# Order of the score visits in a hybrid attention layer: pattern 1 in front of the joint pattern, with a new table of priority shifts

## The chip, the cores and the metric

The kernel runs on one core of a Trainium2 chip. The core has TensorE (PE in the profile, PEld its weight loads), VectorE (DVE), ScalarE (ACT), GpSimd (POOL) and SyncE (SP), which here issues nearly all DMAs. The metric is the device time of one execution in microseconds; lower is better. Before the change the median of three runs is 1198.13 us.

## The reference, cut to what matters

One decoder layer on x of 2048 tokens by 1024 columns. A norm and an input projection give q, k, v and a gate for 12 heads of 64, and the four inputs of a gated convolution of width 256. Each head attends in three dilated windows, whose outputs are combined by the softmax of their log-sums:

```python
DILATED_PATTERNS = ((128, 1), (512, 4), (2048, 16))
...
for window, dilation in DILATED_PATTERNS:
    o_i, lse_i = dilated_window_attn(q, k, v, window, dilation)
...
mix_w = jax.nn.softmax(jnp.stack(lses, axis=0), axis=0)
o = jnp.sum(mix_w[..., None] * jnp.stack(outs, axis=0).astype(jnp.float32), axis=0)
attn_out = o.astype(x.dtype).reshape(B, S, ATTN_WIDTH) * jax.nn.silu(g_attn)
```

Both groups, concatenated, go through an output projection and a second norm and are added to x.

## The kernel before

**Work and units.** The 2048 tokens are four blocks of 512 (`NB = 4`). The projection's columns are eight groups: group 0 and group 7 hold the convolution, groups 1 to 6 one pair of heads each. The program walks over n = 0 to 31, group n // 4 and block n % 4. Each n is a projection (L925 to L936: 96 matmuls of 128x128 by 128x512, three products of split operands for each of eight steps of depth and four outputs, into the z banks of PSUM) and a unit: `conv_unit` for the convolution or `attn_unit` for a pair of heads. There are 24 attention units; the texts number them 0 to 23, so unit u is pair u // 4, block u % 4. After them comes the output projection, done as a two-by-two product with seven multiplications (from L948 on).

**An attention unit.** q and k are copied from PSUM by ACT (L608), swapped by halves of 32 rows with eight DMAs (L611), and turned by the rotary tables on DVE and POOL (L623, L627). The turned q is split in two parts in Q (L638, L639) and copied by POOL in another order of tokens into Q1 (L643). v is scaled by DVE (L615), transposed by PE (L655), split (L660, L662), sent to DRAM and read back in the order that the pattern of dilation 1 needs (L667, L670).

**Scores.** Two kinds of scores are made. The patterns of dilation 4 and 16 share one set, the joint pattern (`score4`, L683 to L706, matmuls at L691, reading Q). The pattern of dilation 1 is pattern 1 (`score1`, L708 to L734, matmuls at L719, reading Q1). Each call makes a group: two st banks of PSUM, one for each head; matmuls; then for each head a DVE pass that adds the mask and takes the extreme of each row (L698, L726) and an ACT pass that takes the exponential and sums the row (L702, L730). The results go into P4 (ring p4, two buffers, one for each head) and P1 (ring p1, two buffers). The extremes and sums of the joint pattern go into sm, those of pattern 1 into E.

The joint pattern has 1, 2, 4 and 4 groups in blocks 0 to 3, pattern 1 has two. Groups are taken two at a time into a **visit** of PE (L806 to L811), so that a unit has 2, 2, 3 and 3 visits. A visit has the score layout of the array, 64 rows of one head beside 64 of the other. There are five st banks.

**After the scores.** First the joint pattern (kind 4) and then pattern 1 (kind 1) is taken, for each head: PE transposes the probabilities (L759; in blocks 2 and 3 DVE transposes a part, L750), ACT and DVE split them (L764, L765), PE multiplies with v (L781), and ACT and DVE gather the outputs (L797 to L799, POOL at L841). In parallel E goes to DRAM and back, since its rows are in the other order of tokens: four DMAs at L847 and one at L849, whose result is X. X and sm are combined on DVE in `w_a` (L857 to L859), ACT (L861) and DVE in `w_b` (L866 to L873); the weights go to DRAM and back (L877, L880), scale the two outputs (L890, L891), and the sum is gated and stored (L892 to L895).

**What sets the order.** Every operation is entered in a plan with an engine, a modelled duration, a priority and what it reads and writes. `schedule` (L199) runs the plan in modelled time: whenever an engine is free it takes the ready operation of the lowest priority number, the one entered first among equals, provided its buffers are free; operations marked with a mode go ahead of others while the engine is in a mode. The program is then written out in the order of the modelled starts, and each engine runs its own part in that order. An operation of unit n has the priority 100 n + 60, or that less 100,000 where it empties a PSUM bank; the projection of n has 100 n + 50. So the projection of the next n fills PE wherever the unit's own work isn't ready. All visits of a unit have the same priority.

`SHIFT` (L117) changes priorities by hand. A key is (hundreds of the priority, site), and a site is the number of the source line that enters the operation, counted in the order in which such lines come up first (L190 to L197).

Of the kernel before, what the change touches and what calls it, by code (L numbers as in the profile page):

```python
# [110 lines left out]
class Op:  # L111
# [3 lines left out]


SHIFT = {  # L117
# [5 lines left out]
}  # L123


class Plan:
# [39 lines left out]
    def add(self, eng, dur, prio, fn, r=(), w=(), after=(), land=None, mode=0, port=False, data=0.0):  # L166
        op = Op()
        op.eng, op.dur, op.prio, op.fn, op.toks = eng, dur, prio, fn, []
        op.start = op.end = None
        op.land = (6.0 if land is None else land) if dur and (eng == "DMA" or land) else 0.0  # L170
        op.n, op.mode, op.port, op.data = len(self.ops), mode, port, data
        if eng == "DMA" and dur > 0.7:

            op.dur, op.data = 0.47, data or dur
        deps = set(after)
        for k in r:
            self._access(op, k, False, deps)
        for k in w:
            self._access(op, k, True, deps)
        deps.discard(op)  # L180
        op.deps = deps
        op.outs = []
        op.wait = len(deps)
        op.ready = 0.0
        for d in deps:
            d.outs.append(op)
        self.ops.append(op)
        return op
# [118 lines left out]
def mmt(n):  # L307
    return max(0.109, n * 0.000433 + 0.0071)


def actt(n, psum=False, ptr=False):
    return n / 1200.0 + (0.05 if psum else 0.093) + (0.093 if ptr else 0.0)
# [5 lines left out]
def dvet(n):  # L318
    return n / 960.0 + 0.067
# [11 lines left out]
def hybrid_layer(ctx: ExitStack, tc: tile.TileContext, x, w_in, w_out, conv_w, g_pre, g_post,  # L331
# [257 lines left out]
    def attn_unit(n, p, b, zs):  # L589
# [15 lines left out]
        for j, c in enumerate("kq"):  # L605
            s, r = Tok(rp_r), Tok(rp_r)
# [3 lines left out]
            for a in (0, 32, 64, 96):  # L610
                add("DMA", 0.63, pe + j, lambda s=s, r=r, a=a: nc.sync.dma_start(r.ap[a:a + 32], s.ap[a ^ 32:(a ^ 32) + 32]),  # L611
                    r=[s], w=[(r, a)], land=2.1, data=0.24)
# [5 lines left out]
        def rotate(c, engines):  # L618
# [21 lines left out]
            r=[q, (Q, 0)], w=[(Q, 1)], port=True)  # L640

        for l in range(2):
            add("POOL", poolt(C) / 2, pr, lambda l=l: pool.tensor_copy(  # L643
                tokens(Q1.ap[:, l]), rows(Q.ap[:, l])),
                r=[(Q, l)], w=[(Q1, l)])
# [15 lines left out]
        for h in range(2):  # L661
            add("DVE", dvet(256), pr + URG, lambda h=h: vec.tensor_tensor(  # L662
                v2.ap[:, :, 1 + h, :], src()[:, :, h, :], f(v2.ap[:, :, 3 * h, :]), op=ALU.subtract),
                r=[ps, (v2, 0)], w=[(v2, 1 + h)])
# [11 lines left out]
        def s4(i, h=None):  # L676
            a = sm.ap[:, 16 * i:16 * i + 8].rearrange("p (h r) -> p h r", h=2)
            return a if h is None else a[:, h]

        P = {}  # L680
        per = (4, 2, 1, 1)[b]

        def score4(r0):  # L683

            ps = [Tok(st_r), Tok(st_r)]

            def qk():
                for r in range(r0, r0 + per):
                    for x, (i, j) in enumerate(products):
                        for h, (lo, hi) in enumerate(halves):  # L690
                            mm(ps[h].ap[:, (r - r0) * w:(r - r0 + 1) * w], Q.ap[lo:lo + 64, i, r * 128:(r + 1) * 128],  # L691
                               KK[j][lo:lo + 64, 4 * r:4 * r + 4, 0:w // 4].rearrange("p s (c a) -> p c s a", a=32), start=x == 0, stop=x == 2)

            def rest():
                for h in range(2):
                    P4 = P[h, 4]
                    for r in range(r0, r0 + per):
                        add("DVE", dvet(w) + 0.01, pr + URG, lambda h=h, r=r, P4=P4: vec.tensor_tensor_reduce(  # L698
                            P4.ap[:, r, 0:w], ps[h].ap[:, (r - r0) * w:(r - r0 + 1) * w], mask4[:, C - w:], 1.0, 3.0e38,
                            op0=ALU.add, op1=ALU.min, accum_out=s4(0, h)[:, r:r + 1]), r=[ps[h], "masks"], w=[(P4, r), (sm, ("m", h, r))])  # L700
                    for r in range(r0, r0 + per):
                        add("ACT", actt(w) + 0.19, pr, lambda h=h, r=r, P4=P4: act.activation(  # L702
                            P4.ap[:, r, 0:w], P4.ap[:, r, 0:w], AF.Exp, bias=s4(0, h)[:, r:r + 1], scale=-1.0,
                            accum_out=s4(1, h)[:, r:r + 1]), r=[(sm, ("m", h, r))], w=[(P4, r), (sm, ("d", h, r))])
            return (3 * per * mmt(w), qk, [Q] + [("kk", j, i) for j in range(b + 1) for i in range(2)],
                    ps + [(P[h, 4], "hold") for h in range(2)], rest)  # L706

        def score1(g0):  # L708
            ps = [Tok(st_r), Tok(st_r)]
            lo = {g: 128 if b == 0 and g == 0 else 0 for g in (g0, g0 + 1)}  # L710

            def qk():
                for j, g in enumerate(lo):
                    k0 = b * 32 + (g - 1) * 8
                    for x, (i, l) in enumerate(products):
                        for h, (p0, _) in enumerate(halves):
                            kk = KK[l][p0:p0 + 64]
                            keys = kk[:, :, k0 + 8:k0 + 16] if lo[g] else kk[:, :, k0:k0 + 16].rearrange("p x (c a) -> p c x a", c=2)
                            mm(ps[h].ap[:, j * 256 + lo[g]:(j + 1) * 256], Q1.ap[p0:p0 + 64, i, g * 128:(g + 1) * 128], keys,  # L719
                               start=x == 0, stop=x == 2)  # L720

            def rest():
                for h in range(2):
                    P1 = P[h, 1]
                    for j, g in enumerate(lo):
                        add("DVE", dvet(256) + 0.01, pr + URG, lambda h=h, j=j, g=g, P1=P1: vec.tensor_tensor_reduce(  # L726
                            P1.ap[:, g, lo[g]:], ps[h].ap[:, j * 256 + lo[g]:(j + 1) * 256], mask1[:, lo[g]:], 1.0, 3.0e38,
                            op0=ALU.add, op1=ALU.min, accum_out=E.ap[:, g, h:h + 1]), r=[ps[h], "masks"], w=[(P1, g), (E, ("m", h, g))])
                    for g in lo:
                        add("ACT", actt(256 - lo[g]) + 0.19, pr, lambda h=h, g=g, P1=P1: act.activation(  # L730
                            P1.ap[:, g, lo[g]:], P1.ap[:, g, lo[g]:], AF.Exp, bias=E.ap[:, g, h:h + 1], scale=-1.0,
                            accum_out=E.ap[:, g, 2 + h:3 + h]), r=[(E, ("m", h, g))], w=[(P1, g), (E, ("d", h, g))])
            return (6 * mmt(256), qk, [Q1] + [("kk", j, i) for j in (max(b - 1, 0), b) for i in range(2)],
                    ps + [(P[h, 1], "hold") for h in range(2)], rest)  # L734
# [67 lines left out]
        for h in range(2):  # L802
            P[h, 4], P[h, 1] = Tok(p4_r), Tok(p1_r)

        groups = [score4(r) for r in range(0, 4, per)] + [score1(g) for g in (0, 2)]
        for i in range(0, len(groups), 2):  # L806
            visit = groups[i:i + 2]
            score_last.append(add("PE", sum(g[0] for g in visit), pr, lambda visit=visit: [g[1]() for g in visit], r=[k for g in visit for k in g[2]],
# [70 lines left out]
        for h in range(2):  # L879
# [3 lines left out]
                r=[ak + (r,) for r in range(4)], w=[(ab, h)], land=8.0, data=1.8)  # L883


        def weight(i):
# [7 lines left out]
            r=[a4, gs], w=[a1], port=True)  # L894
# [17 lines left out]
    for n in range(8 * NB):  # L912
# [30 lines left out]
        if grp in (0, 7):  # L943
            conv_unit(n, grp // 7, b, zs)
        else:
            attn_unit(n, grp - 1, b, zs)
# [259 lines left out]
```

## Time and the profile before

| what | value |
|---|---|
| median of three runs | 1198.13 us (1196.64 to 1198.43) |
| the profiled execution: its time | 1198.13 us |
| the profiled execution: span from the first to the last instruction | 1196.3 us |
| mean granted clock of TensorE | 0.999 |
| ACT busy | 716.1 us, 60% |
| POOL busy | 265.2 us, 22% |
| DMA: data moved, mean rate | 280.46 MB, 234 GB/s |

Times in the profile count from the first instruction. A line such as L691 is a line of the kernel printed above. A row of a group or a timeline names the engine, the line, the operation, the tile that is written, an arrow, the tiles that are read, the shape and the count; in square brackets stands the idle time in front of the instruction and what ended it. Matmuls are pipelined and their ends are modelled, so the distance between starts says more than a duration. A tile's name comes without its buffer number, so st is any of the five score banks.

### The profile page before, as it was taken

The page shows a single profiled execution, that of the slowest core. Times are in us where ns is not written, and L with a number is a line of the kernel's source. Part 1 is how long each engine was busy: PE and PEld are TensorE (multiplying, and loading weights), DVE is VectorE, ACT ScalarE, POOL GpSimd, SP SyncE. Part 2 cuts the span into 40 slices and gives each one's busy share as a digit, 9 for nine tenths or more (in the row PEclk, how much of TensorE's full clock was granted, in tenths as well). Part 3 has the DMA queues.
Part 4 walks back from the last instruction along what each step waited for, and adds up shares of the span by engine and source line. Part 5 has one row for each costly group of instructions (what it writes and reads, how often), then busy time and mean ns, then how long its engine had stood idle before and what let it go on. Part 6 is the DMA issues. An engine that isn't in the chain of part 4 may idle for free.

```text
span 1196.3 us, 20842 instructions
## 1 busy us (share of the span) xinstructions
PE 1182.5 (99%) x6716; PEld 981.9 (82%) x6716; DVE 922.5 (77%) x2331; ACT 716.1 (60%) x1875; POOL 265.2 (22%) x212
## 2 busy tenths in 40 slices
PE   9999999999999999999999999999999999999997
PEld 7788888888888888888878888888888888888886
DVE  4665478787779977786878867798877899787876
ACT  7433457656757676675857766576767563454443
POOL 0011123322223232222332232232332213100000
PEclk9999999999999999999999999999999999999999
DMA  9989766786768867777768777778657978635452
GB/s 342 371 324 360 247 217 213 251 245 221 213 212 261 255 203 238 215 239 216 231 214 246 235 217 228 222 250 274 225 168 228 318 225 335 203 124 192 139 172 89
DMA packets 175294, 280.46 MB, mean 234 GB/s; under 512 B 53712, under 2 KB 109776, under 8 KB 175184
## 3 DMA queue, kind: packets, MB, share of 16 engines
q1 hardware_dynamic: 174896, 278.86, 72.3%
q8 instruction: 53, 0.87, 0.3%
q14 instruction: 57, 0.47, 0.1%
q10 hardware_dynamic: 288, 0.27, 0.1%
HBM read 215.42 MB, written 51.05 MB: 223 GB/s over the span
## 4 chain that ended last, share of the span: by engine, by line
PE 87%; DMA 5%; DVE 3%; ACT 2%; issue 1%; SPq 1%; DVEq 0%; ACTq 0%
PE z L933 17%; PE z L935 16%; PE z L934 16%; PE st L781 8%; PE st L759 5%; PE st L691 4%; PE st L719 3%; PE st L1100 3%; PE st L1099 3%; PE st L1101 3%; PE z L1101 2%; PE z L1099 2%; PE z L1100 2%; DMA ex<-ed 1%; PE st L933 1%
## 5 line engine op out<-in xcount | busy, mean ns | idle before, releaser
L933 PE MATMUL z<-xt,w 128*128 128x512 f32 x960 | 391.0, 407 | 0.7 <-DVE rp L558 0.4
L935 PE MATMUL z<-xt,w 128*128 128x512 f32 x960 | 376.1, 392 | 0.0
L934 PE MATMUL z<-xt,w 128*128 128x512 f32 x960 | 375.5, 391 | 0.2 <-DVE xt L493 0.2
L933 PEld LDWEIGHTS z<-xt,w 128*128 128x128 f32 x960 | 180.7, 188 | 39.4 <-issue 7.5
L935 PEld LDWEIGHTS z<-xt,w 128*128 128x128 f32 x960 | 180.1, 188 | 39.9
L934 PEld LDWEIGHTS z<-xt,w 128*128 128x128 f32 x960 | 180.9, 188 | 29.7 <-DVE xt L493 0.5
L702 ACT ACTIVATE p<-p,sm 128x128 f32<-128x128 f32 (+3 forms) x192 | 105.7, 553 | 64.1 <-DVE sm L698 64.1
L781 PEld LDWEIGHTS st<-pt,v 128*128 128x128 f32 x852 | 118.2, 190 | 17.4 <-DVE pt L765 4.5
L781 PE MATMUL st<-pt,v 128*128 128x256 f32 x852 | 128.1, 286 | 3.4 <-DVE pt L765 3.2
L765 DVE TENSOR_TENSOR pt<-st,pt 128x512 fp32r<-128x512 f32 (+1 forms) x180 | 116.7, 675 | 16.6 <-ACT pt L764 14.9
L799 DVE TENSOR_TENSOR uu<-st,uu 64x256 f32<-64x256 f32 x192 | 79.5, 420 | 58.4 <-ACT uu L798 44.9
L797 ACT COPY uu<-st 64x256 f32<-64x256 f32 x192 | 69.5, 367 | 66.0 <-PE st L781 55.8
L764 ACT CAST pt<-st 128x512 fp32r<-128x512 f32 (+1 forms) x180 | 98.3, 579 | 14.6 <-PE st L759 12.1
L841 POOL TENSOR_TENSOR uu<-uu 128x512 f32<-128x512 f32 x48 | 69.3, 1443 | 158.8 <-DVE uu L799 139.3
L730 ACT ACTIVATE p<-p,e 128x256 f32<-128x256 f32 (+1 forms) x192 | 94.7, 497 | 15.8 <-DVE e L726 15.8
L698 DVE CUSTOM_DVE_ANT_0 p<-st,cst 128x128 f32<-128x128 f32 (+3 forms) x192 | 81.9, 486 | 28.1 <-PE st L691 27.7
L759 PE MATMUL st<-cst,p 128*128 128x128 f32 x708 | 98.3, 273 | 0.0
L759 PEld LDWEIGHTS st<-cst,p 128*128 128x128 f32 x708 | 82.5, 140 | 11.8 <-issue 1.2
L623 POOL TENSOR_TENSOR rp<-rp,cs 128x512 f32<-128x512 f32 x24 | 36.2, 1509 | 216.7 <-DMA rp<-rp 96.0
L798 ACT COPY uu<-st 64x256 f32<-64x256 f32 x192 | 68.7, 367 | 18.6 <-PE st L781 13.2
L726 DVE CUSTOM_DVE_ANT_0 p<-st,cst 128x256 f32<-128x256 f32 (+1 forms) x192 | 66.9, 410 | 13.9 <-PE st L719 13.6
L623 DVE TENSOR_TENSOR rp<-rp,cs 128x512 f32<-128x512 f32 x72 | 53.8, 764 | 20.4 <-DMA rp<-rp 18.8
(315 smaller groups left out, 1912.7 us busy)
## 6 DMA issues: line engine op xcount, KB each, us to landing
xt<-xt SPq DMA_DIRECT2D x256, 512.0 KB
cs<-t SPq DMA_DIRECT2D x28, 768.0 KB
raw<-in_w_in SPq DMA_DIRECT2D x58, 256.0 KB
rp<-rp SPq DMA_DIRECT2D x192, 64.0 KB
vd<-v SPq DMA_DIRECT2D x24, 512.0 KB
v<-vd SPq DMA_DIRECT2D x96, 128.0 KB
ab<-ad SPq DMA_DIRECT2D x48, 256.0 KB
uu<-mix SPq DMA_DIRECT2D x27, 256.0 KB
```

The lines of the kernel that those rows point to most:

```text
L623: add(e, dur, pr, lambda o=o, a=a, i=i, eng=eng: eng.tensor_tensor(o.ap, a.ap, cs.ap[:, i], op=ALU.mult), r=[cs], w=[o], port=True)
L698: add("DVE", dvet(w) + 0.01, pr + URG, lambda h=h, r=r, P4=P4: vec.tensor_tensor_reduce(P4.ap[:, r, 0:w], ps[h].ap[:, (r - r0) * w:(r - r0 ...
L702: add("ACT", actt(w) + 0.19, pr, lambda h=h, r=r, P4=P4: act.activation(P4.ap[:, r, 0:w], P4.ap[:, r, 0:w], AF.Exp, bias=s4(0, h)[:, r:r + ...
L730: add("ACT", actt(256 - lo[g]) + 0.19, pr, lambda h=h, g=g, P1=P1: act.activation(P1.ap[:, g, lo[g]:], P1.ap[:, g, lo[g]:], AF.Exp, bias=E ...
L759: nc.tensor.transpose(ps.ap[:, i * 128:(i + 1) * 128], pp.ap[:, a, c * 128:(c + 1) * 128], ident)
L764: add("ACT", actt(m * 128, True), pr + URG, lambda: act.copy(pt.ap[:, :m, 0, :], p4()), r=[ps], w=[(pt, 0)])
L765: add("DVE", dvet(m * 128), pr + URG, lambda: vec.tensor_tensor(pt.ap[:, :m, 1, :], p4(), f(pt.ap[:, :m, 0, :]), op=ALU.subtract), r=[ps, ...
L781: mm(dst, v, pt.ap[:, i], start=s, stop=e)
L799: add("DVE", dvet(256), pr + URG, lambda: vec.tensor_tensor(cols(a, lo), o()[lo:lo + 64, 0], cols(a, lo), op=ALU.add), r=[O], w=[(a, (h, h ...
L933: mm(z.ap, w.ap[:, 0, js], xt.ap[:, 0], start=kt == 0, stop=False)
L934: mm(z.ap, w.ap[:, 0, js], xt.ap[:, 1], start=False, stop=False)
L935: mm(z.ap, w.ap[:, 1, js], xt.ap[:, 0], start=False, stop=kt == KT - 1)
```

## The change

The list of groups is built with pattern 1's two groups first; the joint pattern's follow. Groups are still taken two at a time, so in every block the first visit now holds both groups of pattern 1. In block 0, where the first visit held the joint pattern's one group and one of pattern 1, the second visit now holds the joint pattern's group alone. The operations that follow a visit are entered in the same new order, which also exchanges the numbers of the sites of L698 and L702 with those of L726 and L730.

The table of shifts is replaced: 54 entries for 37, of which 17 are the same as before, one is changed and 36 are new; 19 are dropped.

```diff
 SHIFT = {
-    (-1, 15): 90, (1, 24): -3, (5, 70): 10, (6, 69): 60, (7, 50): 30, (8, 50): 30, (9, 66): -3, (11, 43): 20,
-    (11, 54): 30, (12, 34): 60, (13, 52): 60, (14, 50): 30, (15, 43): -30, (15, 49): -3, (15, 70): 30, (16, 67): -10,
-    (16, 70): -30, (17, 72): 3, (18, 45): -3, (18, 50): 3, (19, 54): 60, (19, 64): 60, (19, 72): 57, (20, 50): 30,
-    (22, 64): 3, (22, 71): 30, (23, 43): 3, (26, 45): -60, (26, 87): -3, (27, 49): -30, (27, 71): -60, (28, 35): -30,
-    (30, 42): 60, (31, 35): -30, (33, 94): -3, (34, 106): -60, (34, 108): -60,
+    (-1, 15): 90, (0, 8): -60, (1, 24): -3, (2, 11): -60, (3, 44): -60, (5, 70): 10, (6, 35): 60, (6, 69): 60,
+    (6, 74): -10, (6, 87): -60, (7, 44): -60, (7, 45): 60, (7, 52): 60, (7, 86): 30, (8, 71): 3, (9, 66): -3,
+    (10, 52): 20, (10, 69): 60, (11, 43): 20, (12, 69): 10, (13, 50): 3, (14, 45): -30, (15, 43): -30, (15, 70): 30,
+    (18, 69): 60, (19, 35): -60, (19, 54): 60, (19, 62): 60, (19, 70): -10, (20, 50): 30, (21, 53): -3, (22, 71): 30,
+    (23, 33): -3, (23, 43): 3, (23, 72): 3, (23, 87): -10, (24, 35): -60, (24, 54): -3, (26, 45): -60, (26, 87): -3,
+    (27, 21): -60, (27, 71): -60, (28, 29): 60, (28, 35): -30, (30, 29): 30, (31, 29): -60, (31, 35): -30,
+    (33, 92): -60, (34, 100): 30, (34, 106): -120, (34, 111): -3, (35, 105): 10, (35, 111): -30, (36, 106): -90,
 }
...
-        groups = [score4(r) for r in range(0, 4, per)] + [score1(g) for g in (0, 2)]
+        groups = [score1(g) for g in (0, 2)] + [score4(r) for r in range(0, 4, per)]
         for i in range(0, len(groups), 2):
             visit = groups[i:i + 2]
```

## The prediction

> **What bounds the kernel now.** I read the page's busy times first, then the table by windows, then the waits of PE, and only then the timelines around the longest of those waits.
>
> ```profile
> span 1196.3 us, 20842 instructions
> PE 1182.5 (99%) x6716; PEld 981.9 (82%) x6716; DVE 922.5 (77%) x2331; ACT 716.1 (60%) x1875; POOL 265.2 (22%) x212
> ```
>
> PE is busy in all but 13.8 us of the span. That figure alone could mislead, since the ends of matmuls are modelled and overlap, so here is a stretch of the timeline of PE, a visit of the joint pattern (L691) with its neighbours; the columns are start, duration, engine, line, operation, tiles, shape, count.
>
> ```profile
> 245.75 0.39 PE L935 MATMUL z<-xt,w 128*128 128x512 f32 x1
> 246.07 1.67 PE L691 MATMUL st<-kk,q 64*128 64x512 f32 x12
> 247.66 0.50 PE L933 MATMUL z<-xt,w 128*128 128x512 f32 x1
> 248.01 0.39 PE L934 MATMUL z<-xt,w 128*128 128x512 f32 x1
> 248.23 0.40 PE L935 MATMUL z<-xt,w 128*128 128x512 f32 x1
> ```
>
> Projection matmuls start about 0.23 us apart although each is drawn 0.39 long: the array is fed without a hole. Going into the score visit costs 0.32 instead of 0.23, and coming out 0.35 instead of 0.23, about 0.2 us for both. So there are two places from which an order could take time: the idle time, and the number of such crossings. The table by windows says where the idle time is (columns: window, its length, then busy time of PE, PEld, DVE, ACT, POOL with counts, then clock, DMA share, GB/s).
>
> ```profile
> 130.00:985.00 855.00, 850.27 (x5204) 709.90 (x5204) 678.15 (x1830) 569.25 (x1586) 238.96 (x191) 1.00 0.75 233
> 985.00:1189.00 204.00, 204.00 (x885) 165.57 (x884) 168.51 (x334) 88.80 (x190) 14.46 (x9) 1.00 0.54 181
> 1189.00:1197.00 8.00, 0.43 (x2) 0.01 (x1) 3.42 (x9) 0.98 (x3) 0.00 (x0) 0.80 0.35 132
> ```
>
> The attention stage, 130 to 985 us, has 855.00 - 850.27 = 4.73 us of idle PE. The output product has none. After the last matmul some 6.9 us (1196.3 less 1189.43, since the last window holds 0.43 of PE) go to norm, scale and store, which the edit of the visits does not touch and no entry of the table of shifts names. The waits of PE itself, complete, are these (engine, tile and line <- what ended the wait: total, times, longest):
>
> ```profile
> PE st L781 <- DVE pt L765: 3.2, 4, 1.5
> PE st L655 <- DVE rp L615: 1.3, 1, 1.3
> PE st L905 <- DVE u L553: 1.1, 1, 1.1
> PE z L933 <- DVE rp L558: 0.4, 1, 0.4
> PE z L933 <- DVE u L559: 0.3, 1, 0.3
> PE z L934 <- DVE xt L493: 0.2, 1, 0.2
> PE st L484 <- DVE xt L493: 0.2, 1, 0.2
> ```
>
> Five waits, 4.5 us, lie in the attention stage (L781 and L655), and all five end on DVE. L905 is the warm-up at the start; the last four rows, 1.1 us, are x's transposes and the first conv units. With the gaps too short to be listed this is the 4.73. An order that hides everything there is worth 4.73 us, 0.39%, and no order is worth more unless it also changes the crossings.
>
> **The change part by part.**
>
> *The same work on PE.* No matmul is added or dropped. The visits stay as many: a pair of heads has, for the four blocks, 2, 2, 3 and 3 visits before and after, 60 in all over six pairs, at 0.2 us a crossing some 12 us. Two full visits need eight st banks of the five there are, so they cannot stand back to back to save a crossing. I cost this at nothing; its bounds are one crossing either way, 0.2 us.
>
> *The wait that pattern 1 starts.* The row maxima and sums of pattern 1 (E) go to DRAM and back, four DMAs at L847 and one at L849, before DVE can combine the patterns (w_a, from L857). With pattern 1 scored last, E is the last thing that a unit makes, and the trip is naked. The longest wait, in unit 2 (pair 0, block 2), first on DVE, then on PE:
>
> ```profile
> 234.59 0.17 DVE L857 TENSOR_TENSOR sm<-ex,sm 128x8 f32<-128x8 f32 x1 [3.39 <-DMA ex<-ed]
> 235.29 0.67 DVE L765 TENSOR_TENSOR pt<-st,pt 128x512 fp32r<-128x512 f32 x1
> ```
> ```profile
> 236.11 0.71 PE L781 MATMUL st<-pt,v 128*128 128x256 f32 x4 [1.52 <-DVE pt L765]
> ```
>
> DVE stands 3.39 us before an instruction of 0.17 us. Queued behind it is the split of a transposed probability tile (L765), and PE waits 1.52 us for that. The trip that ended so late, on ACT (the last sum of pattern 1), on SP's queue, and in the chain of work:
>
> ```profile
> 218.54 0.20 ACT L730 ACTIVATION_READ_ACCUMULATOR p<-p,e 128x1 f32 x1
> ```
> ```profile
> 217.19 5.01 SPq L611 DMA_DIRECT2D rp<-rp  x8
> 222.87 2.50 SPq L847 DMA_DIRECT2D ed<-e  x4
> ```
> ```profile
> 224.83 4.80 DMA ed<-e
> 229.71 4.86 DMA ex<-ed
> ```
>
> E is complete at 218.74 and X is there at 234.57: 15.8 us, of which 222.87 - 218.74 = 4.1 are SP issuing the eight rotation DMAs of the next unit first, so 11.7 without them. The two visits stand this far apart, and Q1, which pattern 1 reads, is ready in time:
>
> ```profile
> 198.68 1.33 PE L691 MATMUL st<-kk,q 64*128 64x384 f32 x12
> 210.30 1.84 PE L719 MATMUL st<-kk,q 64*128 64x256 f32 x24
> ```
> ```profile
> 197.64 0.62 POOL L643 CAST q<-q 128x512 fp32r<-128x512 f32 x1 [1.88 <-DVE q L639]
> ```
>
> Put in front, pattern 1's visit goes up by 11.6 us, E is complete near 207.1, and X is there at 207.1 + 11.7 = 218.8, with the SP delay at 222.9. The sums of the joint pattern, which w_a needs too, now come last, about where E's came, 218.7. So DVE's wait falls from 3.39 to between 0.1 and 4.2 us at a place 11.7 us earlier; I take the low end, because the rotation DMAs are issued from 217.19 and E's issues now come ahead of them. PE's 1.52 us goes with it.
>
> The Trainium skill ("DMA: Bandwidth & Descriptors", section "Latency and other measured facts") puts the fixed cost of one DMA at about 2 us, which two DMAs and 2.5 us of issue would make a trip of about 6.5 us, an estimate; by it the lead would cover every unit and the sum below would hold with no remainder. The trace disagrees: 4.80 and 4.86 us for transfers of a few KB.
>
> Where blocks are short the lead is shorter. Unit 13 (pair 3, block 1), from the chain of work, then DVE, then PE:
>
> ```profile
> 588.72 1.64 PE st L691 x24
> 594.66 1.80 PE st L719 x24
> ```
> ```profile
> 615.85 1.04 DVE L857 TENSOR_TENSOR sm<-ex,sm 128x8 f32<-128x8 f32 x1 [0.34 <-DMA ex<-ed]
> 617.01 1.27 DVE L859 TENSOR_TENSOR sm<-sm,sm 128x8 f32<-128x8 f32 x1
> 618.77 0.69 DVE L615 TENSOR_TENSOR rp<-z,cs 128x512 f32<-128x512 f32 x1
> ```
> ```profile
> 619.52 0.66 PE L655 MATMUL st<-cst,rp 128*128 128x128 f32 x4 [1.31 <-DVE rp L615]
> ```
>
> Here the lead is 5.94 us, less than the trip of 11.7, so a wait of up to 5.8 us can stay on DVE in the blocks 0 and 1 if w_a is put where the sums of the joint pattern end. What cost PE its 1.31 us was w_a landing late and slow in front of L615, which PE's transposes need. Over all units:
>
> ```profile
> DVE sm L857 <- DMA ex<-ed: 9.6, 7, 3.4
> ```
> ```profile
> L857 DVE TENSOR_TENSOR sm<-ex,sm x24: 149/167/1255, 159.6 to 971.0; 128x8 f32<-128x8 f32 x24
> ```
>
> Of seven such waits only these two reached PE, and at a median of 0.167 us the 1.04 is an exception. With w_a at least 5.94 us earlier it no longer stands between this L615 and its reader. The bounds of this term are 0 and -1.31; I take -1.31, being nearer to the median row than to the slow one, and keep 0 for the range.
>
> *What comes later instead.* The joint pattern's probabilities are made 5 to 6 us later in a unit, and their transposes and products with v are the first to follow. The cover is the projections of the next unit, which fill PE between all visits above; PE has no wait of its own for L691's or L719's readers in the list. I cost it at nothing; without that cover it would be a wait like the third below. P1 is now held from the first visit to the last transposes, and has one buffer per head, but in unit 2 those transposes are over before the next unit's visit at 246.07 (PE's last wait for them ends at 236.11). Nothing.
>
> *The new table of shifts.* It has 54 entries for 37, 17 of them unchanged, and moves priorities by 3 to 120 units; which buffers and waits follow I cannot read from it. Bounds: everything gone, 4.73 us, and the rivals below. In the output product there is no wait to lose or win.
>
> **Sum.** The profiled run took 1198.13 us, 1.8 more than its span, and is itself the median. 1198.13 - 1.52 - 1.31 = **1195.3 us**.
>
> **Rivals.**
>
> *The waits change place.* DVE's waits of other kinds stay, and a new order deals anew which of them reach PE: 4.73 us over 24 units is 0.2 us a unit, and a new draw of the same size gives 1198.1. For it speaks that the other three waits at L781 (3.2 - 1.5 = 1.7 us) have nothing to do with E. The change can also fail to do what it says: visits of a unit share one priority, and the first that is ready goes, so the joint pattern, which does not need Q1, can still go first. Then E is no earlier and the time is again 1198.1. Against it: Q1's copy takes 0.62 us and is done at 198.26, before the visit.
>
> *E's DMAs in the way of the rotation (slower).* SP issues in order. E's four issues hold the queue 2.5 us; put ahead of the eight rotation DMAs of the next unit they make L623 on DVE wait that much. The trace has such a case, DVE and then PE:
>
> ```profile
> 601.82 1.29 DVE L623 TENSOR_TENSOR rp<-rp,cs 128x512 f32<-128x512 f32 x2 [2.69 <-DMA rp<-rp]
> ```
> ```profile
> 603.77 0.74 PE L781 MATMUL st<-pt,v 128*128 128x256 f32 x4 [0.78 <-DVE pt L765]
> ```
>
> 2.69 us on DVE became 0.78 on PE. From 2.83/0.78 = 3.6 units on it eats the gain, and from about 6.7 units on the kernel is slower by over 2.4 us; at 8 units it is 1195.3 + 6.2 = 1201.5. For it: in unit 2 E's issues change sides with exactly those DMAs. Against: they are then over by 210, before 217.19, and the rotation DMAs have the higher priority in the planner.
>
> *Everything hidden.* 1198.13 - 4.73 = 1193.4 us.
>
> **How the numbers follow.** 0.2%, 2.4 us, is about what a measurement of this kernel can tell from no change; that is below 1195.7 or above 1200.5. Forecast 0.45, waits that change place 0.30, slower 0.17, everything hidden 0.08. The forecast lies just beyond the mark, and with the L655 term at zero it is 1196.6, within it; I give 0.33 of its 0.45 to faster. Faster 0.33 + 0.08 = 0.41, same 0.12 + 0.30 = 0.42, slower 0.17. The likeliest case's own range is 1194.5 to 1196.8. The range for 8 in 10 starts at 1193.0, everything hidden with 0.4 of the start's small waits, and ends at 1200.5, which leaves out most of the slower case.
>
> **What would show it.** L719 starts in front of L691 in each unit. DVE's wait for ex falls below 9.6 - 3.4 = 6.2 us in total. PE's wait at L781 falls to about 1.7 and the one at L655 is gone; PE idles about 2 us between 130 and 985, and 6.9 after the last matmul as now. PE's busy time stays within 1 us of 1182.5. I am wrong if PE's idle time in that stage is 4 us or more, if DVE waits longer for rp (L623), or if the busy time moves.

## The result, and the profile after

The changed kernel takes 1211.17 us (median of three, 1211.08 to 1211.32), the kernel before 1198.13: a ratio of 1.011, with a 95% interval of 1.0094 to 1.0126. It is slower by 13 us; the forecast was 1195.3 with a range of 1193.0 to 1200.5. Ratios here are taken over fast runs and need not equal the quotient of two medians.

In the changed kernel every line from L127 on stands two lines further down: L691, L719, L759, L781, L857 of before are L693, L721, L761, L783, L859. First the page's busy times, then the table by windows (columns as before).

```profile
span 1209.4 us, 20813 instructions
PE 1187.0 (98%) x6716; PEld 983.3 (81%) x6716; DVE 933.6 (77%) x2331; ACT 714.6 (59%) x1875; POOL 265.4 (22%) x212
```
```profile
130.00:985.00 855.00, 844.35 (x5133) 701.85 (x5132) 673.89 (x1808) 559.76 (x1569) 238.78 (x190) 1.00 0.73 231
985.00:1202.00 217.00, 215.52 (x959) 175.32 (x957) 182.62 (x358) 96.97 (x206) 15.10 (x10) 1.00 0.54 179
```

The work on PE is the same 6716 matmuls. PE idles 1209.4 - 1187.0 = 22.4 us where it idled 13.8. Of the 8.6 us more, 10.65 - 4.73 = 5.9 lie in the attention stage and 1.5 after it; the rest is at the start and at the end. PE's busy time grew by 4.5 us with the same work. About 1.7 of that is a stretch at half clock (last section). Another part is drawing: a matmul is drawn 0.39 us long while the next could start after 0.23, so each wait hides 0.16, and the list has 21 waits for 10, which makes some 1.8 (an estimate). About 1 us of the 4.5 stays open. The longest waits, and two of DVE's:

```profile
PE st L783 <- DVE pt L767: 4.4, 9, 0.9
PE st L783 <- DVE e L728: 3.3, 3, 1.8
PE z L935 <- DVE rp L560: 1.5, 1, 1.5
PE st L783 <- ACT p L704: 1.3, 1, 1.3
```
```profile
DVE sm L859 <- DMA ex<-ed: 15.8, 10, 3.2
DVE rp L625 <- DMA rp<-rp: 14.4, 9, 4.2
```

PE's waits before the products with v are 4.4 + 3.3 + 1.3 = 9.0 us (L783) where they were 3.2 (L781). DVE's wait for X, which the change was forecast to shorten, grew from 9.6 to 15.8 us. The wait for the rotation DMAs, on which the slower rival rested, is there, but total 14.4 us is no sign of new trouble: the list of before has 18.8 for L623.

**The visits.** Unit 2, of which the prediction gave the visits before, in the timeline of PE after:

```profile
198.74 1.34 PE L693 MATMUL st<-kk,q 64*128 64x384 f32 x12
204.78 1.84 PE L721 MATMUL st<-kk,q 64*128 64x256 f32 x24
210.18 1.34 PE L693 MATMUL st<-kk,q 64*128 64x384 f32 x12
```

The joint pattern still goes first, and pattern 1 second. Over all units, pattern 1 starts first in 12 of 24, and in none of block 0, where it is turned round altogether. Unit 8 (pair 2, block 0), before and then after, with the last product of the unit:

```profile
424.02 1.56 PE L691 MATMUL st<-kk,q 64*128 64x128 f32 x24
425.42 0.95 PE L719 MATMUL st<-kk,q 64*128 64x128 f32 x12
429.23 1.04 PE L719 MATMUL st<-kk,q 64*128 64x256 f32 x12
...
444.62 0.52 PE L781 MATMUL st<-pt,v 128*128 128x256 f32 x3
```
```profile
416.20 1.56 PE L693 MATMUL st<-kk,q 64*128 64x128 f32 x24
432.88 1.38 PE L721 MATMUL st<-kk,q 64*128 64x128 f32 x18
...
448.23 0.51 PE L783 MATMUL st<-pt,v 128*128 128x256 f32 x3
```

The joint pattern's lone group, two banks, runs early, and pattern 1's visit, four banks, 16.7 us later. The unit takes 32.0 us from its first score to its last group of products where it took 20.6. Such spans of all 24 units, from the timelines of PE, starts to starts, average 30.2 us before and 34.4 after. The part from a unit's last score matmul to its last product grew from 20.6 to 23.0. The attention stage has some 855/24 = 35.6 us for each unit, so on average the units follow each other with 5.4 us to spare before and 1.2 after. In blocks 2 and 3 a unit is longer than 35.6 us in both kernels (35.8 and 39.7 before, 38.8 and 42.2 after), and there it can run into the next.

**DVE beside POOL.** The rotation's products on DVE (line, means in ns), before and after:

```profile
L623 DVE TENSOR_TENSOR rp<-rp,cs 128x512 f32<-128x512 f32 x72 | 53.8, 764 | 20.4 <-DMA rp<-rp 18.8 <-ACT p L730 1.0 <-ACT p L702 0.5
```
```profile
L625 DVE TENSOR_TENSOR rp<-rp,cs 128x512 f32<-128x512 f32 x72 | 63.3, 894 | 14.5 <-DMA rp<-rp 14.4
```

Those 72 instructions take 9.5 us more, most of the 11.1 by which DVE's busy time grew. Where it comes from is seen ahead of PE's longest wait. DVE, then POOL, then PE:

```profile
854.06 0.69 DVE L893 TENSOR_TENSOR uu<-uu,ab 128x512 f32<-128x512 f32 x1
854.67 2.37 DVE L625 TENSOR_TENSOR rp<-rp,cs 128x512 f32<-128x512 f32 x2
857.07 1.67 DVE L629 TENSOR_TENSOR rp<-rp,rp 128x512 f32<-128x512 f32 x1
858.67 1.76 DVE L625 TENSOR_TENSOR rp<-rp,cs 128x512 f32<-128x512 f32 x1
```
```profile
854.83 1.66 POOL L894 TENSOR_TENSOR uu<-uu 128x512 f32<-128x512 f32 x1 [0.81 <-DVE uu L893]
856.57 1.63 POOL L895 TENSOR_TENSOR uu<-uu,g 128x512 f32<-128x512 f32 x1
858.16 1.73 POOL L625 TENSOR_TENSOR rp<-rp,cs 128x512 f32<-128x512 f32 x1
```
```profile
861.04 0.51 PE L783 MATMUL st<-pt,v 128*128 128x256 f32 x2 [1.77 <-DVE e L728]
```

Alone, such an instruction takes 0.69 us. Started while POOL works it takes 1.67 or 1.76 and ends 0.54 us after POOL's. DVE reaches L728 at 860.35, and PE stands 1.77 us.

### The profile page after: what moved, and what is told of

Read it like the earlier page. It is cut to its first block, busy times and chain, and to the rows that moved or that the text cites. A ratio compares the mean times of both kernels' runs of the same rounds, so it can differ in the third digit from the quotient of the medians.

```text
span 1209.4 us, 20813 instructions
## 1 busy us (share of the span) xinstructions
PE 1187.0 (98%) x6716; PEld 983.3 (81%) x6716; DVE 933.6 (77%) x2331; ACT 714.6 (59%) x1875; POOL 265.4 (22%) x212
## 4 chain that ended last, share of the span: by engine, by line
PE 77%; DVE 9%; ACT 5%; DMA 5%; issue 2%; SPq 1%; DVEq 0%; POOL 0%; ACTq 0%
PE z L935 14%; PE z L937 14%; PE z L936 14%; PE st L783 7%; PE st L761 5%; PE st L693 3%; PE st L1103 3%; PE st L1102 3%; PE st L1101 3%; PE st L721 3%; DVE rp L625 2%; PE z L1102 2%; PE z L1103 2%; PE z L1101 2%; DMA ex<-ed 2%
## 5 line engine op out<-in xcount | busy, mean ns | idle before, releaser
L783 PEld LDWEIGHTS st<-pt,v 128*128 128x128 f32 x852 | 118.3, 190 | 26.8 <-DVE pt L767 10.4
L783 PE MATMUL st<-pt,v 128*128 128x256 f32 x852 | 130.1, 288 | 9.3 <-DVE pt L767 4.4
L766 ACT CAST pt<-st 128x512 fp32r<-128x512 f32 (+1 forms) x180 | 98.2, 579 | 20.6 <-PE st L761 18.9
L761 PE MATMUL st<-cst,p 128*128 128x128 f32 x708 | 97.8, 274 | 0.0
L761 PEld LDWEIGHTS st<-cst,p 128*128 128x128 f32 x708 | 83.5, 141 | 11.7 <-issue 0.7
L728 DVE CUSTOM_DVE_ANT_0 p<-st,cst 128x256 f32<-128x256 f32 (+1 forms) x192 | 66.5, 410 | 14.0 <-PE st L721 13.7
L625 DVE TENSOR_TENSOR rp<-rp,cs 128x512 f32<-128x512 f32 x72 | 63.3, 894 | 14.5 <-DMA rp<-rp 14.4
```

Source lines behind the costliest of these rows:

```text
L625: add(e, dur, pr, lambda o=o, a=a, i=i, eng=eng: eng.tensor_tensor(o.ap, a.ap, cs.ap[:, i], op=ALU.mult), r=[cs], w=[o], port=True)
L761: nc.tensor.transpose(ps.ap[:, i * 128:(i + 1) * 128], pp.ap[:, a, c * 128:(c + 1) * 128], ident)
L766: add("ACT", actt(m * 128, True), pr + URG, lambda: act.copy(pt.ap[:, :m, 0, :], p4()), r=[ps], w=[(pt, 0)])
L783: mm(dst, v, pt.ap[:, i], start=s, stop=e)
```

## The experiments

Theory C: the joint pattern's probabilities are used first; scored last, their transposes and products start late, every unit is longer, and PE feels it. Rivals: T, the new table costs; X, E's trip; P, DVE beside POOL.

**Order and table apart.** The kernel before with an empty table (e1), the changed one with an empty table (e2), the kernel before with the new table (e3, its keys 62 and 64 exchanged back). The fourth combination, the changed order with the old table, was not run.

```diff
-SHIFT = {
-    (-1, 15): 90, (1, 24): -3, (5, 70): 10, ...
...
+SHIFT = {}
```

> The old order of the visits with an empty table of shifts. Theory C (cover: the joint pattern's probabilities are used first, so scoring them last lengthens every unit, and the projections that fill PE run out): the order itself is good and the table only polishes it, so 1199 to 1206 us, well under the 1211 of the changed kernel. Theory T (the new table is what costs): also 1199 to 1206; alone it does not tell them apart, it is the base of the next two.

> The new order of the visits with an empty table of shifts. Theory C: slower than the old order without a table by at least the 13 us of the whole change, 1214 us or more, since the new table was made to repair it. Theory T: the order is harmless, so within 3 us of the old order without a table.

> The old order with the new table; the two sites that the order renumbers are put back on their operations. Theory T: the loss is here, 1209 us or more. Theory C: a table made for another order fits badly, so some loss against 1198, but the table without the order gives back at least a part: 1200 to 1208 us, under the changed kernel.

Then, both without a table, the use turned round: pattern 1's probabilities are transposed and multiplied first.

```diff
-        for kind in (4, 1):
+        for kind in (1, 4):
```

> The new order without a table, and pattern 1's probabilities are also transposed and multiplied first (the loop over kinds is turned round), so that what is scored first is used first. Theory C: the loss of the new order without a table shrinks by at least half. Theory T and a theory that E's trip or the order of visits alone costs: no change, within 3 us of the new order without a table.

> The old order of the visits without a table, with the loop over kinds turned round: now the joint pattern is scored first and used last, and pattern 1, scored last, is used first. Theory C (what is used first must be scored first): slower than the old order without a table (1203.6 us) by 4 us or more, 1207.5 or above. Theory K (using pattern 1 first is simply better, whatever is scored first): 1203.6 or below.

| kernel | median us | ratio to before, 95% interval | unit, first score to last product | last score to last product | PE idle, 130 to 985 us |
|---|---|---|---|---|---|
| before | 1198.1 | | 30.2 | 20.6 | 4.7 |
| changed | 1211.2 | 1.011 [1.0094, 1.0126] | 34.4 | 23.0 | 10.7 |
| e1 joint listed first, used first | 1203.6 | 1.0047 [1.0028, 1.0065] | 30.6 | 20.8 | 6.3 |
| e2 pattern 1 listed first, joint used first | 1214.7 | 1.0112 [1.0078, 1.0147] | 33.8 | 23.4 | 15.0 |
| e3 as e1, new table | 1200.3 | 1.0011 [0.9991, 1.003] | 30.1 | 20.5 | 3.7 |
| e4 pattern 1 listed first, used first | 1203.7 | 1.0032 [1.0015, 1.0048] | 32.9 | 21.6 | 7.7 |
| e5 joint listed first, pattern 1 used first | 1212.0 | 1.0116 [1.0095, 1.0138] | 34.5 | 24.3 | 6.4 |

Theory T falls: the new table on the old order is 1.0011, not to be told from the kernel before. The order costs by itself, 0.65% (8 us by the ratios, 11 by the medians) without tables. e4 and e5 are the sharpest pair: neither "joint first" nor "pattern 1 first" is good by itself. What is listed first has to be used first; each mismatch costs some 0.65% by the ratios and each match is near 1203.6. The time from the last score to the last product goes with it; the whole unit does not, for e4's 32.9 us is nearer to e2's 33.8 than to e1's 30.6. PE doesn't follow the list in every unit: pattern 1 starts first in 10 of 24 units in e2, 11 in e4 and 1 in e5. Of theory C's five expectations four held; e2 passed its 1214 us, but lay 11 us over e1, not 13.

The two mismatches lose their time in different places, by the profiles. From e1 to e2 PE's idle time in the attention stage grows by 8.7 us, and e4 takes 7.3 of it away again; e2's profile, of an execution of 1219.35 us, also has 3.4 us of lost clock. In e5 the idle time there is that of e1. The profile of e5 shows instead one long wait of PE, at 1019 us, for the convolution behind the last attention unit, and two stretches of half clock (last section), near 851 us and right behind that wait:

```profile
PE z L928 <- DVE rp L553: 5.3, 1, 5.3
```
```profile
851.00:859.00 8.00, 6.16 (x20) 5.16 (x20) 6.36 (x29) 4.89 (x23) 3.47 (x4) 0.57 0.99 352
1022.00:1029.00 7.00, 4.57 (x11) 3.60 (x12) 5.14 (x10) 1.25 (x2) 1.61 (x1) 0.51 0.20 60
```

The clock column makes that 8 x 0.43 + 7 x 0.49 = 6.9 us of lost clock. So e5 shows that its mismatch is slow, and not that its units leave PE idle; how the order of use leads to that wait stays open.

**By blocks.** The old order without a table, with pattern 1 listed in front in some blocks alone:

```diff
-        groups = [score4(r) for r in range(0, 4, per)] + [score1(g) for g in (0, 2)]
+        fours, ones = [score4(r) for r in range(0, 4, per)], [score1(g) for g in (0, 2)]
+        groups = ones + fours if b == 0 else fours + ones
```

(e12: `b > 1`.)

> The old order without a table, but in block 0 pattern 1 goes first. Theory C: block 0 is only one of the places; 3 to 7 us over the old order without a table (1203.6), 1206 to 1211. Theory D (all of the loss is block 0, where pattern 1's visit now needs four banks and ran 14 us after the joint pattern's in the changed kernel): 1212 to 1216.

> The old order without a table, but in blocks 2 and 3 pattern 1 goes first. Theory C: there the time from the last visit to the last product grew from 24.1 to 26.9 and from 26.2 to 29.8 us in the changed kernel, so most of the loss is here: 1209 to 1215. Theory D: within 3 us of 1203.6.

Block 0 alone gave 1207.6 us (1.0082 [1.0059, 1.0105]), blocks 2 and 3 alone 1214.2 (1.0134 [1.0112, 1.0156]), against 1.0047 for neither. Theory D falls: block 0 costs some 4 us, blocks 2 and 3 some 10. Together they would be more than e2, so the parts do not add. In block 0 the mechanism is not simply the order: in all six units of e11's block 0 the joint pattern still starts first and ends first. There the edit moves a group of pattern 1 out of the joint pattern's visit into a visit of four banks, and the unit takes 31.8 us where e1's takes 20.6, with 14.2 from its last score to its last product, not more than e1's 14.6. Block 1 alone wasn't run.

**What of it reaches PE, in the changed kernel.** The next kernels keep the order of the kernel that they start from on every engine and take work out, so they leave out a part of the sums. e6 lets the combination read the joint pattern's numbers, so that DVE never waits for X; e7 cuts POOL's sums to 32 columns (128 in the last two); e8 does both.

```diff
-            m1 = X.ap[:, :, 0:2].rearrange("p r h -> p h r")
+            m1 = s4(0)
...
-            d1 = X.ap[:, :, 2:4].rearrange("p r h -> p h r")
+            d1 = s4(1)
```
```diff
-lambda a=a, t=t: pool.tensor_tensor(a.ap, a.ap, t.ap, op=ALU.add)
+lambda a=a, t=t: pool.tensor_tensor(a.ap[:, 0:32], a.ap[:, 0:32], t.ap[:, 0:32], op=ALU.add)
...
```

> The changed kernel with the same order of instructions, in which the combination on DVE reads the joint pattern's numbers in place of those of pattern 1, so that DVE never waits for X; E's DMAs are still issued. It leaves out pattern 1's row extremes and sums. Theory X (E's trip, which the profile shows as 15.8 us of waits on DVE, is the cost): back to 1202 us or less. Theory C: the wait for X reached PE in three places (about 1.5, 1.1 and 1.0 us start to start at 397, 404 and 546 us), so 1 to 4 us off 1211.2, not more: 1207 to 1210.

> The changed kernel with the same order of instructions, in which POOL's part of q's rotation and the sum of each pattern's two halves are done on 32 of 512 columns, and the last sum and gating on 128 of 512, so that POOL is hardly ever busy beside DVE. It leaves out the rest of those sums. Theory P (DVE instructions stretched beside POOL are the cost; the rotation on DVE takes 0.894 us on average against 0.764 before): 1203 us or less, since the longest wait, at 859 us, and the half clock after it go too. Theory C: only a part, 3 to 7 us: 1204 to 1208.

> Both at once on the changed kernel, same order of instructions; leaves out what the two leave out. Theories X and P together, with no cost in the order itself: at or below the kernel before, 1198 us or less. Theory C: the order as written out has PE wait for chains that are long even so; 1202 us or more.

> The kernel before with POOL's sums cut as in the changed kernel with the short POOL; it leaves out the same parts. Theory C with slack (a unit of the kernel before takes about 30 us from its first scores to its last product, one of the changed kernel 34, and PE has 36 us of work a unit, so before the same stretched DVE instructions are mostly absorbed): it gains at most its own idle time, 1 to 5 us, 1193 to 1197. Theory P alone (the 12 us that the short POOL gives the changed kernel are simply the price of POOL beside DVE, in any order): about 12 us here too, 1186 to 1188.

> The kernel before with both cuts, leaving out what they leave out. Theory C with slack: 1193 to 1196 us, so that with DVE's delays taken away both orders cost the same to within 3 us (the changed one gave 1195.5). Theory O (the changed order makes PE do more or cross more often by itself): a difference of 5 us or more stays.

| taken away | changed kernel | kernel before |
|---|---|---|
| nothing | 1211.2, 1.011 | 1198.1 |
| wait for X | 1209.1, 1.0084 [1.0069, 1.0099] | not run |
| most of POOL's sums | 1199.4, 1.0011 [0.9996, 1.0025] | 1192.9, 0.9959 [0.9945, 0.9974] |
| both | 1195.5, 0.9977 [0.9966, 0.9988] | 1192.5, 0.9954 [0.9939, 0.9968] |

Theory X gets 2 us, with intervals that overlap. PE's idle time from 130 to 985 us is 10.6 us in e6 against 10.7, so most of the 2 us may be the 1.7 of the half clock, which e6's profile does not have. Theory P expected 1203 or less and got 1199.4, while C had expected 1204 or more, and 1202 or more for both cuts: two misses. So C as first put, long chains that PE waits for whatever DVE does, falls. With these delays of DVE gone the changed order is only 0.23% behind the old one, 3.1 us by the medians. But the same cut is worth 12 us in the changed kernel and 5 in the kernel before, where P alone had expected 12 in both. e9 and e10 came out just under the 1193 that theory C named, and its 3 us between the two orders were just passed. The kernel before has many of the same delays and hides most. What the order takes away, by this, is the room to hide them.

**Stretched, or late?** The short POOL also has its results ready sooner. So each cut sum is followed by two fills (e13) or three (e14), which keep POOL busy and read nothing:

```diff
+    def pool_less(out, a, b, op, head, rest):
+        pool.tensor_tensor(out[head], a[head], b[head], op=op)
+        for _ in range(2):
+            pool.memset(out[rest], 0.5)
...
```

> The changed kernel, same order of instructions, with each of the cut sums of POOL followed by two plain fills of the columns left out, so that POOL stays busy but reads little; it leaves out the sums. Theory S (DVE instructions are stretched while POOL reads beside them): DVE's rotation stays near 0.70 us on average, as with the short POOL, and if POOL's instructions with their fills take 1.4 us again, the time stays near 1199, at most 1203. Theory L (what helped was that POOL's results came sooner): back to 1208 to 1211.

> The same with three fills, so that the two bracket the time that POOL takes in the changed kernel (265.4 us busy). Theory S: near 1199, at most 1205 where the fills make POOL longer than it was. Theory L: 1208 or more, and later than with two fills.

e13 took 1198.5 us (1.0004 [0.9995, 1.0014]), e14 1202.6 (1.0035 [1.0014, 1.0056]). Engines of e13, and its rotation on DVE:

```profile
PE 1181.3 (99%) x6716; PEld 983.2 (82%) x6716; DVE 890.8 (74%) x2331; ACT 714.5 (60%) x1875; POOL 263.5 (22%) x500
```
```profile
L632 DVE TENSOR_TENSOR rp<-rp,cs 128x512 f32<-128x512 f32 x72 | 49.8, 707 | 14.2 <-DMA rp<-rp 13.9 <-issue 0.2
```

POOL is busy 263.5 us against 265.4, and the 12.7 us are back all the same. DVE does the same instructions in 890.8 us instead of 933.6. With three fills POOL is busy 341.8 us, far more than it was, and the kernel is still 9 us faster than the changed one. Theory L falls: it is the stretching. The 43 us by which POOL stretches DVE in the changed kernel cost it 12; the 33.6 us in the kernel before (922.5 less the 888.9 that e9 shows) cost it 5, by the short POOL alone, for the fills were not run there.

Whether the 8 to 11 us between e1 and e2 would vanish in the same way was not tried. Their DVE is busy nearly alike, 923.8 and 922.6 us, so more stretching is not the cause there; less room for as much of it would fit, and is not shown.

## Why the prediction was wrong

*Same work on PE:* right in its count, wrong in saying that PE's busy time stays within 1 us: it rose by 4.5, about 1.7 from the half clock, some 1.8 from waits drawn as work, and the rest open.

*What comes later instead, costed at nothing:* the step that failed. The joint pattern's products were moved back and their cover was taken to be the projections, because PE had no wait for them in the profile of before. What the runs showed instead is not one wait but less room: on average a unit takes 4.2 us more from its first score to its last product, 2.4 of them behind its last score, against a spare of 5.4 us. Delays of DVE that this room had swallowed then show on PE, whose waits before the products grew from 3.2 to 9.0 us. e1 to e5 show that the order, of scoring against use, is the cause, in block 0 (e11) with the visits put together anew, and e7, e9 and e13 that delays of DVE beside POOL are what comes through. That the room is the link between the two is argued from the lengths of the units and fits e7 and e9; no run changes the room alone.

*E's trip:* the lead was mis-sized. It counted pattern 1's visit as two visits earlier; the plan put it one visit earlier in unit 2 and last in unit 8, perhaps because the joint pattern was ready sooner, or needed two banks where pattern 1 needed four; neither was tested. The prediction had this as a way in which the change fails, at no cost. Where pattern 1 did go first, the lead fell short. Unit 7, the last sums of pattern 1 and of the joint pattern on ACT, the trip, then DVE and PE:

```profile
389.91 0.19 ACT L732 ACTIVATION_READ_ACCUMULATOR p<-p,e 128x1 f32 x1
...
398.56 0.19 ACT L704 ACTIVATION_READ_ACCUMULATOR p<-p,sm 128x1 f32 x1
```
```profile
394.38 2.90 DMA ed<-e
397.37 5.54 DMA ex<-ed
```
```profile
402.94 0.17 DVE L859 TENSOR_TENSOR sm<-ex,sm 128x8 f32<-128x8 f32 x1 [1.90 <-DMA ex<-ed]
```
```profile
404.97 0.98 PE L783 MATMUL st<-pt,v 128*128 128x256 f32 x6 [0.91 <-DVE pt L767]
```

The lead is 398.75 - 390.10 = 8.65 us, the trip 12.8, the wait 1.90, and PE loses 0.91. The 11.7 us of the prediction was a fair size for the trip. The figure of the Trainium skill ("DMA: Bandwidth & Descriptors", section "Latency and other measured facts"), 2 us for each DMA, is again too small (2.90 and 5.54). The prediction's trip of 6.5 us by that figure would not have been covered in every unit either, since unit 13 has a lead of 5.94. The whole term is worth at most some 2 us (e6), with the sign turned round, and little of it as idle time of PE.

*The table:* bounded by the waits there were to lose; it did no harm (e3).

*The bounds:* "no order is worth more than 4.73 us" limits the gain. The loss was bounded by one rival only, E's DMAs ahead of the rotation's, and that did not come. A change that moves what 24 units do needed a bound from the room per unit. The rows for it were there: lengths of units in the timeline, and DVE instructions of 1.04 and 1.27 us beside a median of 0.167, which the prediction called an exception.

## What to carry to other kernels

Where a filler keeps one engine busy, its short list of waits does not say that the other engines have time; measure how long a unit of the dependent work takes, the whole of it and the part behind its last score, since here neither alone followed the time, and how much of the filler's time that leaves. Score first what is used first: of two stages with the same work, turn round both orders or neither. And look at instructions that take twice their median while another engine works, since a tighter order can make the kernel pay for them.

## What the runs showed of the hardware

A DVE instruction on two SBUF tensors, 128x512 in f32, takes 0.69 us alone and up to 1.76 when POOL has started a tensor_tensor; beside POOL's fills it stays at 0.707 on average over 72 (e13). The Trainium skill ("SBUF — State Buffer", section "Who interferes with whom") says that a DVE instruction with two SBUF inputs contends with a GpSimd instruction that reads SBUF and not with one that only writes; the runs agree on both.

In the changed kernel a wait of PE of 1.77 us was followed by half clock on TensorE. The table by windows around it, with the granted clock third from the end:

```profile
860.00:862.00 2.00, 0.96 (x5) 0.87 (x6) 2.00 (x12) 1.51 (x8) 1.29 (x1) 0.98 0.96 288
862.00:864.00 2.00, 2.00 (x9) 1.72 (x8) 2.00 (x9) 1.95 (x8) 0.00 (x0) 0.50 0.70 281
864.00:866.00 2.00, 2.00 (x10) 1.61 (x9) 0.78 (x3) 1.88 (x7) 0.00 (x0) 0.67 0.27 47
```

The clock is half in all of 862 to 864 and in part of the windows beside it, 0.08 + 2.0 + 1.32 = 3.4 us, which costs 1.7 us of matmuls. The length of the wait does not decide it alone. e6 has the same wait, and the clock stays full behind it:

```profile
860.18 0.50 PE L783 MATMUL st<-pt,v 128*128 128x256 f32 x2 [1.77 <-DVE e L728]
```
```profile
862.00:864.00 2.00, 2.00 (x14) 1.69 (x13) 1.41 (x5) 1.90 (x8) 0.00 (x0) 1.00 0.57 176
```

Nor did a wait of 2.08 us in e13 and those of 1.52 and 1.31 in the kernel before bring it. The Trainium skill ("TensorE: Matmul & The Clock Gate", section "What's actually happening") has the clock fall after an idle window of about 3.4 us; in the changed kernel PE was idle for 1.8 of the 3.4 us before the fall, with matmuls at both ends, so here less was enough. Which waits bring it, no run here settles. It differs between runs of one kernel: e14's ten go from 1198.29 us at a mean granted clock of 0.999 to 1210.90 at 0.996.
